# Feed-forward stages of a hybrid encoder layer: all engines but GpSimd in the source's order, a pair's products regrouped, loads two pairs ahead

## The chip, the cores and the metric

The kernel runs on one core of one Trainium2 chip. Times are microseconds on the device, of one execution of the whole layer; lower is better. Five engines work side by side, each with its own queue of instructions: TensorE (PE, with its weight loads as PEld) multiplies matrices, VectorE (DVE) and ScalarE (ACT) do elementwise work, GpSimd (POOL) here raises to a power, copies a little and issues the transfers that add onto their destination, and SyncE (SP) issues the other transfers. They meet only through semaphores: an instruction that waits holds everything behind it on its own engine.

## The reference, cut to what matters

One encoder layer: x is 512 positions by 1024 channels, F is 2752.

```
x = x + 1/2 * SwiGLU_1(RMSNorm(x))
h = RMSNorm(x); u = h @ w_in
x = x + concat([fourier(u), attention(u)]) @ w_out
x = x + 1/2 * SwiGLU_2(RMSNorm(x))
y = RMSNorm_final(x)

SwiGLU(h) = (silu(h @ w_gate) * (h @ w_up)) @ w_down
```

The change touches the two SwiGLU networks alone. Each holds three matrix products of 512 x 1024 x 2752 (gate, up, down).

## The kernel before, in words

Everything is float32, computed as a high part (rounded to the type fp32r that TensorE takes at full rate) and a low remainder; a product is three matmuls: high x high, high x low, low x high. So each weight block that comes in is first cast by ScalarE (the high part) and then subtracted by VectorE (the low part, `lows`, L119).

F is cut into 21 blocks of 128 columns and a tail of 64. Block j of gate and block j of up make pair j. Of each network the first three or four pairs and the tail ("plain", function `gate`, L272) are multiplied in the usual way. The other 17 or 18 pairs go through `seven`, L379: gate and up of a pair are the two column halves of one product, and this product is done in Strassen's manner (Winograd's form) with seven half-sized products in place of eight. For these, VectorE first builds sums of the weight quarters (a11, a12, a22 are quarters; s1 to s4 are sums of them, L368) and, once per network, of the activations (b11 to t4, `operands`, L297). One of the seven products is 12 matmuls of 128 x 256 (`multiply`, L389). Results land in three half banks per pair, called r, q and p: r takes a11, then s2, then s3, then a22, each added onto what is there, and between them ScalarE copies the value out (`kept`, L402, the copy is L404); q takes s1, then s4; p takes a12.

In `seven` the order on TensorE is a11, a12, a22 of the pair before, s1, s2, s4, s3 (`step` 0, 1, 9, 3, 4, 5, 6, L407). `prepare`, L336, issues the loads of the next pair: two half loads into tile s (L344, L345), gate into raw_g (L346), an adding transfer from GpSimd that adds up onto s (L347), and the second half of up into raw_u (L348), a buffer of the pool that the down weights also use. Then come six steps of conversion, of which `PIECES` says how many follow each product: casts of raw_g and s (`both`, L351, cast at L353), of raw_u (`single`, L359, cast at L362), sums, cast of the new s. Tiles raw_g and s have two buffers each. The loads of a pair are issued at the first product of the pair before it.

High and low parts lie in a ring of 12 slots; a slot is taken in the source's order and becomes free when the last product of its quarter is done (`take`, `give`, L325, L331).

At the end of a pair (`step` 9, L436) r is evacuated, gate goes through silu, is multiplied with up and stored as high and low part in `at`, one of seven places (L442, L119).

The network runs in four groups of blocks: group 0 holds the plain pairs, and groups 1 to 3 six or seven blocks each. Before the down products of a group its pairs are multiplied, one block ahead; then, for each of eight blocks d of output channels, the group's part of the down product is done (`down`, L461, 18 matmuls of 128 x 512 for six blocks), added to x with factor 1/2 (`residual`, L481), and the first pair of the next group is prepared alongside (`ahead`). The down weights of block d are loaded and cast when d comes up. The last pair of a group is finished (`rest`) after d = 0.

What sets the order: within `in_order` (L111) the instructions of TensorE and SyncE stand in the order of the source; those of ScalarE, VectorE and GpSimd are placed by the tool's own scheduler, which plays the program through with estimated durations. The mixing stage in between has its order written out by hand for all five engines (`ORDER`, L40).

Of the kernel before, what the change touches and what calls it, by code (L numbers as in the profile page):

```python
# [30 lines left out]
USES = "a11", "a12", "s1", "s2", "s4", "s3", "a22"  # L31
PIECES = (0, 1, 1, 1, 2, 1, 0)
# [48 lines left out]
def encoder(ctx, tc, A, out):  # L81
# [32 lines left out]
    def run(steps):  # L114
        for _, f, a in steps:
            f(*a)
# [134 lines left out]
    def ffn(norm, after, wgu, wd, wdt, groups, opening, closing):  # L251
# [6 lines left out]
        with tc.tile_pool(name=f"act{n_}", bufs=1) as ap, tc.tile_pool(name=f"sums{n_}", bufs=2) as sp:  # L258
# [38 lines left out]
            def operands(rp, i0, i1):  # L297
                for i in range(i0, i1):
# [7 lines left out]
                    t = sp.tile([P, 4, HALF], F32, tag="s", name=f"t{n_}_{i}")  # L306
# [18 lines left out]
            def take():  # L325

                pool = own or shared
                taken.append(pool.pop(0))
                return taken[-1]
# [6 lines left out]
            def prepare(j):  # L336
# [4 lines left out]
                a11, a12, a22 = g[:, :S], g[:, S:], u[:, :S]  # L341
                s3, s1 = s4, s2 = t[:, :S], t[:, S:]
                gate, up = wgu[2 * j], wgu[2 * j + 1]
                nc.sync.dma_start(out=s3.rearrange("p (a b) -> p a b", b=P), in_=gate[:, :KH])  # L344
                nc.sync.dma_start(out=s1.rearrange("p (a b) -> p a b", b=P), in_=up[:, :KH])  # L345
                nc.sync.dma_start(out=g.rearrange("p (a b) -> p a b", b=P), in_=gate)  # L346
                nc.gpsimd.dma_start(out=t.rearrange("p (a b) -> p a b", b=P), in_=up, accum_op=ALU.add)  # L347
                nc.sync.dma_start(out=a22.rearrange("p (a b) -> p a b", b=P), in_=up[:, KH:])  # L348
                w = {}

                def both(names, src):  # L351
                    hi, lo = (take() for _ in range(2))
                    nc.scalar.copy(hi, src)  # L353
                    lows(lo, src, hi)
                    for i, n in enumerate(names):
                        w[n] = tuple(t[:, i * S : (i + 1) * S] for t in (hi, lo))
                    w[max(names, key=USES.index), "slots"] = hi, lo

                def single(n, src):  # L359
                    t = take()  # L360
                    hi, lo = t[:, :S], t[:, S:]
                    nc.scalar.copy(hi, src)  # L362
                    lows(lo, src, hi)
                    w[n] = hi, lo
                    w[n, "slots"] = (t,)

                def add(out, a, b):
                    nc.vector.tensor_tensor(out=out, in0=a, in1=b, op=ALU.add)  # L368

                return w, [  # L370
                    (both, ("a11", "a12"), g),
                    (both, ("s3", "s1"), t),
                    (single, "a22", a22),
                    (add, s2, s1, a11),
                    (add, s4, a12, s2),
                    (both, ("s4", "s2"), t),
                ]

            def seven(js, done):  # L379

                done = [done]
                banks = {}
# [24 lines left out]
                def step(j, w, n):  # L407
                    b = banks.setdefault(j, {})
                    if n == 0:
                        b["r"] = bank(f"r{n_}_{j}")[:, :HALF]  # L410
                        multiply(b["r"], "a11", "b11", w, True, j == js[0])
                        b["p1"] = kept(b["r"], "p1", j)
                    elif n == 1:
                        ps = bank(f"p2{n_}_{j}")[:, :HALF]
                        multiply(ps, "a12", "b21", w, True)
                        b["g"] = tp.tile([P, S], F32, tag="g", name=f"g{n_}_{j}")
                        nc.vector.tensor_tensor(out=b["g"][:, HALF:], in0=ps, in1=b["p1"], op=ALU.add)
                    elif n == 3:
                        b["q"] = bank(f"q{n_}_{j}")[:, :HALF]
                        multiply(b["q"], "s1", "t1", w, True)  # L420
                        b["p5"] = kept(b["q"], "p5", j)
                    elif n == 4:
                        multiply(b["r"], "s2", "t2", w, False)
                        b["u2"] = kept(b["r"], "u2", j)
                    elif n == 5:
                        multiply(b["q"], "s4", "b22", w, False)
                        nc.vector.tensor_tensor(out=b["g"][:, :HALF], in0=b["q"], in1=b["u2"], op=ALU.add)
                        nc.scalar.activation(b["g"], b["g"], AF.Silu)
                    elif n == 6:
                        multiply(b["r"], "s3", "t3", w, False)  # L430
# [15 lines left out]
                for s in range(7 * len(js)):  # L446
                    i, n = divmod(s, 7)
                    if n == 2 and i:
                        step(js[i - 1], done[i - 1][0], 9)
# [37 lines left out]
            for gi, group in enumerate(groups):  # L487
# [64 lines left out]
                for f, *a in ahead:  # L552
                    f(*a)
# [891 lines left out]
```

## Time and profile before

| what | value |
|---|---|
| runs before | 881.05, 882.48, 878.42 us, median 881.05 |
| profiled execution | 876.78 us, of which the span from the first to the last instruction is 875.0 |
| granted TensorE clock, mean | 0.995 |
| TensorE busy in the span | 843.4 us, 96% |
| VectorE, ScalarE, GpSimd busy | 606.8, 468.4, 62.5 us |
| DMA | 116.78 MB, 133 GB/s in the mean |

How to read the lines of the profile: times are microseconds from the start of the span, means of one instruction are nanoseconds. A group's line reads: line of the kernel, engine, operation, tile written <- tiles read, shape, count | busy time, mean of one | idle time of the engine just before, and what ended it. A wait's line reads: engine and line that waited <- what ended the wait: us in total, times, longest. A timeline's line reads: start, length, engine, line, operation, tiles, shape, how many were merged, and in brackets the idle time before and its releaser. A window's line gives the busy time of PE, PEld, DVE, ACT and POOL with their instructions in brackets, the granted clock, the busy share of the DMA engines and GB/s. Matmuls overlap: the start of the next one tells more than the length. The feed-forward networks fill the span up to about 345 us and again from 514 us on; the first pair stage of the first network, for example, runs from 77.6 to 136 us, and the down products after it to 172 us.

### The profile page before, as it was taken

The numbers are of one execution on the slowest core, as the hardware profiler recorded it, in microseconds if no ns is written. First come the engines' busy times: TensorE is split into PE (matmuls) and PEld (weight loads), VectorE is DVE, ScalarE is ACT, GpSimd is POOL, SyncE is SP. The second block draws the span as 40 slices with busy tenths as digits, with TensorE's granted clock in tenths as the row PEclk, the third lists the DMA queues.
The fourth block names the chain that finished last, engine by engine and source line by source line (L and its number), as shares of the span: only waits on it lengthen the run. The fifth ranks groups of instructions, "written<-read, shape, count | busy, mean of one in ns | idle before, by whom it ended". The sixth has DMA issues, their size and how long they took to land.

```text
span 875.0 us, 13923 instructions
## 1 busy us (share of the span) xinstructions
PE 843.4 (96%) x5440; PEld 756.8 (86%) x5440; DVE 606.8 (69%) x937; ACT 468.4 (54%) x781; POOL 62.5 (7%) x70
## 2 busy tenths in 40 slices
PE   9999999999899999999999999999999998999996
PEld 7878988899789998889988888799979997899886
DVE  6986876378646747699997479877745865377453
ACT  7754653266524644677774457366523653266352
POOL 0110000001000000122000001000000000000001
PEclk9999999999999999999999999999999999999998
DMA  6677772757364613414110334787454763747112
GB/s 241 172 161 197 191 202 73 187 141 208 80 185 104 158 55 109 145 49 133 49 49 25 97 105 97 195 193 205 121 159 109 190 159 90 188 125 191 46 61 96
DMA packets 46544, 116.78 MB, mean 133 GB/s; under 512 B 5392, under 2 KB 11024, under 8 KB 46352
## 3 DMA queue, kind: packets, MB, share of 16 engines
q1 hardware_dynamic: 38400, 92.05, 33.2%
q0 software_dynamic: 7536, 23.34, 15.6%
q8 instruction: 42, 0.69, 0.3%
q10 hardware_dynamic: 544, 0.52, 0.2%
q14 instruction: 22, 0.18, 0.1%
HBM read 111.44 MB, written 2.10 MB: 130 GB/s over the span
## 4 chain that ended last, share of the span: by engine, by line
PE 76%; DMA 9%; DVE 6%; ACT 4%; issue 2%; SPq 2%; POOL 0%; POOLq 0%; DVEq 0%; ACTq 0%
PE r L396 14%; PE dn L158 8%; PE dn L157 7%; PE dn L156 7%; DMA raw_u<-in_wgu 7%; PE q L396 6%; PE p L396 4%; DVE ring L119 4%; PE mix L156 3%; PE mix L158 3%; PE mix L157 3%; PE gu L156 3%; PE gu L157 2%; PE gu L158 2%; ACT ring L353 2%
## 5 line engine op out<-in xcount | busy, mean ns | idle before, releaser
L396 PE MATMUL r<-rt,ring 128*128 128x256 f32 x1686 | 212.8, 279 | 12.5 <-ACT u L404 12.4
L396 PEld LDWEIGHTS r<-rt,ring 128*128 128x128 f32 x1686 | 202.4, 189 | 16.0 <-ACT u L404 15.1
L156 PE MATMUL dn<-at,ring 128*128 128x512 f32 x300 | 117.6, 392 | 6.9 <-ACT ring L148 6.9
L158 PE MATMUL dn<-at,ring 128*128 128x512 f32 x300 | 117.8, 393 | 3.4 <-DVE ring L119 3.4
L157 PE MATMUL dn<-at,ring 128*128 128x512 f32 x300 | 116.9, 390 | 0.0
L482 DVE SCALAR_TENSOR_TENSOR gx<-dn,gx 128x512 f32<-128x512 f32 x61 | 42.0, 690 | 96.9 <-PE dn L158 96.9
L396 PE MATMUL q<-rt,ring 128*128 128x256 f32 x840 | 106.7, 276 | 0.0
L353 ACT CAST ring<-s 128x1024 fp32r<-128x1024 f32 x70 | 73.6, 1051 | 61.0 <-PE p L396 26.6
L119 DVE TENSOR_TENSOR ring<-s,ring 128x1024 fp32r<-128x1024 f32 x70 | 85.6, 1223 | 27.1 <-ACT ring L353 26.8
L396 PEld LDWEIGHTS q<-rt,ring 128*128 128x128 f32 x840 | 100.5, 188 | 0.0
L148 ACT CAST ring<-raw_dn 128x768 fp32r<-128x768 f32 (+3 forms) x58 | 45.2, 785 | 92.6 <-PE dn L157 78.0
L156 PEld LDWEIGHTS dn<-at,ring 128*128 128x128 f32 x300 | 56.3, 188 | 19.6 <-ACT ring L148 8.5
L158 PEld LDWEIGHTS dn<-at,ring 128*128 128x128 f32 x300 | 56.3, 188 | 18.7 <-DVE ring L119 7.3
L157 PEld LDWEIGHTS dn<-at,ring 128*128 128x128 f32 x300 | 56.3, 188 | 11.3
L347 POOL DMA_DIRECT2D s<-in_wgu x35 | 30.1, 861 | 466.9 <-DVE ring L119 199.8
L119 DVE TENSOR_TENSOR ring<-raw_dn,ring 128x768 fp32r<-128x768 f32 (+3 forms) x58 | 51.5, 894 | 14.1 <-ACT ring L148 13.0
L119 DVE TENSOR_TENSOR ring<-raw_g,ring 128x1024 fp32r<-128x1024 f32 x35 | 42.9, 1226 | 24.5 <-PE p L396 19.0
L396 PE MATMUL p<-rt,ring 128*128 128x256 f32 x420 | 53.6, 277 | 0.0
L396 PEld LDWEIGHTS p<-rt,ring 128*128 128x128 f32 x420 | 50.6, 189 | 0.0
L353 ACT CAST ring<-raw_g 128x1024 fp32r<-128x1024 f32 x35 | 36.5, 1042 | 21.5 <-DMA raw_g<-in_wgu 20.3
L362 ACT CAST ring<-raw_u 128x512 fp32r<-128x512 f32 x35 | 21.7, 621 | 38.0 <-DMA raw_u<-in_wgu 18.9
L119 DVE TENSOR_TENSOR ring<-raw_u,ring 128x512 fp32r<-128x512 f32 x35 | 24.1, 688 | 16.1 <-ACT ring L362 13.8
(308 smaller groups left out, 1543.0 us busy)
## 6 DMA issues: line engine op xcount, KB each, us to landing
s<-in_wgu SPq DMA_DIRECT2D x70, 256.0 KB, 3.5
raw_g<-in_wgu SPq DMA_DIRECT2D x35, 512.0 KB, 5.3
s<-in_wgu POOLq DMA_DIRECT2D x35, 512.0 KB, 6.2
raw_dn<-in_wd SPq DMA_DIRECT2D x40, 384.0 KB, 3.3
raw_u<-in_wgu SPq DMA_DIRECT2D x35, 256.0 KB, 5.5
raw_gu<-in_wgu SPq DMA_DIRECT2D x12, 512.0 KB, 3.5
raw_o<-in_wo SPq DMA_DIRECT2D x8, 512.0 KB, 3.6
raw_dn<-in_wd SPq DMA_DIRECT2D x8, 448.0 KB, 3.7
```

Source lines behind the costliest of these rows:

```text
L119: nc.vector.tensor_tensor(out=lo, in0=src, in1=asf(hi), op=ALU.subtract)
L148: nc.scalar.copy(hi[:, :n, :], raw[:, :n, :])
L156: nc.tensor.matmul(ps, whi, mhi, start=first, stop=False)
L157: nc.tensor.matmul(ps, whi, mlo, start=False, stop=False)
L158: nc.tensor.matmul(ps, wlo, mhi, start=False, stop=last)
L347: nc.gpsimd.dma_start(out=t.rearrange("p (a b) -> p a b", b=P), in_=up, accum_op=ALU.add)
L353: nc.scalar.copy(hi, src)
L362: nc.scalar.copy(hi, src)
L396: nc.tensor.matmul(ps[:, c], a[:, ks], b[:, i, c], start=first and i == 0 and o == 0, stop=i == KH - 1 and o == 2, skip_group_check=not fi ...
L482: nc.vector.scalar_tensor_tensor(out=x[d][:, t], in0=ps[:, t], scalar=0.5, in1=x[d][:, t], op0=ALU.mult, op1=ALU.add)
```

## The change

All of it lies in `ffn`, in `evacuate`, and in one parameter of the program.

Order: `in_full_order` puts ScalarE and VectorE into the source's order as well, in the pair stages and in the loop over d of every group. GpSimd stays with the scheduler. The source is rewritten so that casts and remainders are calls of their own (`Pair.high`, `Pair.low`) and stand between the products where they are to run.

Products: a pair's order on TensorE becomes a11, s1, a12, s2, a22 of the pair before, s4, s3.

Loads: pair i + 2 is loaded at the first product of pair i. Tile s gets a third buffer, raw_u two buffers of its own of half the size. The area for the descriptors of GpSimd's transfers is halved to 8192 bytes.

Down weights: those of d = 0 are cast inside the last pair (`tail(0)`), those of d = 1 after its last product (`tail(1)`), the others two to four blocks ahead (`more_downs`). Some pairs near the end of a stage take slots of the shared part of the ring first (`late`), so that these are free in time.

Groups: in the loop over d the next group's first pair is loaded at d = 0 and its second at d = 4; the first is converted in five portions at d = 3 to 7 (`steps`). The left-over plain pair of group 0 is evacuated in three parts at d = 0, 1 and 2 (`yield` in `evacuate`).

```
-USES = "a11", "a12", "s1", "s2", "s4", "s3", "a22"
-PIECES = (0, 1, 1, 1, 2, 1, 0)
+USES = "a11", "s1", "a12", "s2", "s4", "s3", "a22"
...
+    def in_full_order():
+        return tc.manual_schedule(engines=ORDERED - {mybir.EngineType.Pool})
...
-                t = sp.tile([P, KD * P], F32, tag="s", name=f"s{n_}_{j}")
-                u = wp.tile([P, KD * P], F32, tag="raw", name=f"raw_u{n_}_{j}")
+                t = sp.tile([P, KD * P], F32, tag="s", bufs=3, name=f"s{n_}_{j}")
...
+                def rest():
+                    u = sp.tile([P, S], F32, tag="raw_u", name=f"raw_u{n_}_{j}")
+                    nc.sync.dma_start(out=blocks(u), in_=up[:, KH:])
...
+                def steps(self):
+                    return [
+                        (),
+                        (),
+                        (),
+                        (self.first_high, lambda: self.low("a11")),
+                        (self.last_high, lambda: self.low("a22")),
+                        (self.sums_high, lambda: self.low("s3")),
+                        (self.more_sums, self.more_high),
+                        (lambda: self.low("s4"),),
+                    ]
...
+                late = {i: names for i, names in ((n - 4, ("s3",)), (n - 3, ("a11",)), (n - 2, ("s3", "s4")))}
...
+                for i, j in enumerate(js):
+                    if i + 2 < n:
+                        pairs.append(Pair(js[i + 2], late.get(i + 2, ())))
+                    p, b = pairs[i], Bank(j, pairs[i].w)
+                    x_ = pairs[i + 1] if i + 1 < n else None
+                    b.p1()
+                    if old:
+                        old.r_rest()
+                        p.low("s4")
+                        p.low("a22")
+                    if i + 2 < n:
+                        pairs[i + 2].load_rest()
+                    b.p5()
+                    if x_:
+                        x_.first_high()
+                        x_.sums_high()
+                    else:
+                        tail(0)
+                    b.p2()
+                    if x_:
+                        x_.low("a11")
+                        x_.low("s3")
+                        x_.more_sums()
+                    b.u2()
+                    if old:
+                        old.last()
+                    if x_:
+                        x_.last_high()
+                        x_.more_high()
+                    if old:
+                        old.both()
+                    b.q()
+                    if old:
+                        old.store()
+                    b.silu()
+                    b.r()
+                    old = b
+                old.r_rest()
+                tail(1)
...
+                more_downs(2 if gi else 3)
+                with in_full_order():
+                    for d in range(KD):
...
+                        if not last and d in (0, 4):
+                            new = Pair(groups[gi + 1][0] + 1 + d // 4)
+                            new.load_rest()
...
+                            residual(d_, ps, every)
+                        more_downs(d + (3 if gi and not last else 4))
+                        if not gi:
+                            next(left_over, None)
+                        elif d == 0:
+                            rest()
+                        for d_, *_ in waiting:
+                            added(d_)
...
-    nc = bacc.Bacc("TRN2", target_bir_lowering=False, num_devices=1)
+    nc = bacc.Bacc("TRN2", target_bir_lowering=False, num_devices=1, dynamic_dma_scratch_size=8192)
```

In the new loop `p1`, `p5`, `p2`, `u2`, `last`, `q` and `r` are the products of a11, s1, a12, s2, a22, s4 and s3 with their evacuation, `both` the product of gate and up, `store` the cast and remainder into `at`, `r_rest` the subtraction that ends the first half of up.

More of the change, by code (lines that the diff above doesn't have):

```diff
@@ L367, in add, with blocks @@
[L367 to L382, printed above, removed]
+                def blocks(t):
+                    return t.rearrange("p (a b) -> p a b", b=P)
```

248 lines of the change are left out of this document (131 added, 117 removed).

## The prediction, on record before the result

> **What bounds the kernel now.** I read the page's first two lines, then TensorE's own waits, then the timeline around the longest of them.
>
> ```profile
> span 875.0 us, 13923 instructions
> PE 843.4 (96%) x5440; PEld 756.8 (86%) x5440; DVE 606.8 (69%) x937; ACT 468.4 (54%) x781; POOL 62.5 (7%) x70
> ```
> ```profile
> PE r L396 <- ACT u L404: 12.4, 10, 2.2
> PE dn L156 <- ACT ring L148: 6.9, 7, 1.2
> PE dn L158 <- DVE ring L119: 3.4, 9, 0.7
> PE dn L158 <- DVE at L119: 0.7, 1, 0.7
> ```
>
> PE is busy 843.4 of 875.0 us, so the most that an order of work can win is the idle remainder, and nearly all of it has these four names: 12.4 + 6.9 + 3.4 + 0.7 = 23.4 us in 10 + 7 + 9 + 1 = 27 waits, all in the feed-forward stages. What one wait costs stands in the PE timeline (start, length, columns as on the page, idle before):
>
> ```profile
> 110.78 1.52 PE L396 MATMUL r<-rt,ring 128*128 128x256 f32 x12
> 112.14 1.52 PE L396 MATMUL q<-rt,ring 128*128 128x256 f32 x12
> 115.81 3.01 PE L396 MATMUL r<-rt,ring 128*128 128x256 f32 x24 [2.15 <-ACT u L404]
> 118.66 1.52 PE L396 MATMUL p<-rt,ring 128*128 128x256 f32 x12
> ```
>
> Undisturbed products of 12 matmuls start every 112.14 - 110.78 = 1.36 us. The third row should have started at 113.50 and started at 115.81, and the one after it (two products later, 2.72 us) at 118.66 instead of 116.22: 2.44 us are lost for an idle time shown as 2.15. So each wait costs its idle time plus 0.29 us (the pipeline's end and refill), and the 27 waits cost 23.4 + 27 x 0.29 = 31.2 us.
>
> What ends this wait is read on ScalarE, and then in the chain that ended last:
>
> ```profile
> 110.98 0.37 ACT L404 COPY p<-q 128x256 f32<-128x256 f32 x1 [0.57 <-PE q L396]
> 114.35 0.62 ACT L362 CAST ring<-raw_u 128x512 fp32r<-128x512 f32 x1 [3.00 <-DMA raw_u<-in_wgu]
> 114.88 0.61 ACT L442 CAST at<-u 128x512 fp32r<-128x512 f32 x1
> 115.40 0.37 ACT L404 COPY u<-r 128x256 f32<-128x256 f32 x1
> ```
> ```profile
> 107.74 6.59 DMA raw_u<-in_wgu
> ```
>
> The copy that PE needs (u<-r, 115.40) stands behind the cast of raw_u and one more, and the cast of raw_u waited 3.00 us for a load issued at 107.74, 6.59 us before. Nothing but its place in ScalarE's queue ties the copy to the load. The second kind of wait is at the passage from the pairs to the down products:
>
> ```profile
> 228.69 1.52 PE L396 MATMUL r<-rt,ring 128*128 128x256 f32 x12
> 231.41 0.50 PE L156 MATMUL dn<-at,ring 128*128 128x512 f32 x1 [1.19 <-ACT ring L148]
> 232.40 0.50 PE L158 MATMUL dn<-at,ring 128*128 128x512 f32 x1 [0.26 <-DVE ring L119]
> 236.16 1.58 PE L396 MATMUL r<-rt,ring 128*128 128x256 f32 x12
> 238.54 0.50 PE L156 MATMUL dn<-at,ring 128*128 128x512 f32 x1 [0.80 <-ACT ring L148]
> 239.53 0.50 PE L158 MATMUL dn<-at,ring 128*128 128x512 f32 x1 [0.26 <-DVE ring L119]
> ```
> ```profile
> 230.53 0.82 ACT L148 CAST ring<-raw_dn 128x768 fp32r<-128x768 f32 x1
> 237.66 0.83 ACT L148 CAST ring<-raw_dn 128x768 fp32r<-128x768 f32 x1 [0.69 <-PE r L396]
> ```
>
> Casts of the down weights run at 230.53 and 237.66, the moment the products that need them should begin; their VectorE remainders cost the two 0.26 us gaps.
>
> A third, hidden loss follows one wait:
>
> ```profile
> 704.03 4.40 PE L396 MATMUL r<-rt,ring 128*128 128x256 f32 x24 [1.83 <-ACT u L404]
> 708.23 1.78 PE L396 MATMUL p<-rt,ring 128*128 128x256 f32 x12
> ```
> ```profile
> 705.40:708.70 3.30, 3.30 (x18) 3.30 (x17) 1.70 (x3) 2.23 (x5) 0.00 (x0) 0.50 0.36 85
> ```
>
> After an idle 1.83 us the granted clock (the column 0.50) is half in this stretch. The 24 matmuls hold up the next product for 708.23 - 704.03 = 4.20 us, where after the wait shown above it was 118.66 - 115.81 = 2.85, and the 12 after them take 1.78 instead of 1.52: 1.35 + 0.26 = 1.6 us.
>
> **The change, part by part.**
> Work is neither added nor removed: the same products, casts, remainders and loads. What moves:
>
> Loads two pairs ahead, own buffers for raw_u, a third for s. A pair's period is 7 x 1.36 = 9.52 us. In the new order SyncE can issue a pair's s loads once the s4 remainder of the pair three before is done, its g once the sums of the pair two before are done, its raw_u once that pair's a22 remainder is done. By the loop worked out below (the fixed order), the sums end about 8.5 us into a period and the cast of g, two periods on, starts about 3 us into its own: 1.0 + 9.52 + 3 = 13.5 us of lead; raw_u has about the same, s more. The load seen took 6.59 us. SyncE's queue waits in this order too (raw_u of one pair stands ahead of s and g of the next, and of the first down weights), but each of those waits ends at least a period before anything behind it is needed; past the end of a stage nothing holds the queue, so the first two pairs of the next stage are loaded during the down products. GpSimd's accumulating loads keep their order. So the 10 waits for a copy go: 12.4 + 10 x 0.29 = 15.3 us. If the cover went, each pair would pay up to the 2.44 us shown.
>
> Down weights: cast and remainder of d = 0 stand inside the last pair, of d = 1 behind its last product, the others two or three d ahead. One d of six blocks is 18 matmuls; 16 of them take from 232.40 to 236.16, 0.23 each, so a d lasts 4.1 us, and a cast and its remainder need 0.82 + 0.96 (next fence). That takes away 6.9 + 3.4 + 0.7 + 17 x 0.29 = 15.9 us. Their cover is the product of the d before; without it 0.82 + 0.96 = 1.8 us for a stage come back.
>
> Source order on ScalarE and VectorE: here sits the price. These engines now do a pair's work in one fixed sequence, and a loop closes over both. The rows:
>
> ```profile
> L417 DVE TENSOR_TENSOR g<-p,p 128x256 f32<-128x256 f32 x35 | 14.8, 421 | 3.6 <-PE p L396 2.8
> L119 DVE TENSOR_TENSOR ring<-raw_g,ring 128x1024 fp32r<-128x1024 f32 x35 | 42.9, 1226 | 24.5 <-PE p L396 19.0 <-ACT ring L353 5.5
> L119 DVE TENSOR_TENSOR ring<-s,ring 128x1024 fp32r<-128x1024 f32 x70 | 85.6, 1223 | 27.1 <-ACT ring L353 26.8
> L368 DVE TENSOR_TENSOR s<-raw_g,s 128x512 f32<-128x512 f32 x35 | 24.2, 691 | 1.0
> L368 DVE TENSOR_TENSOR s<-s,raw_g 128x512 f32<-128x512 f32 x35 | 24.0, 687 | 0.2
> L353 ACT CAST ring<-s 128x1024 fp32r<-128x1024 f32 x70 | 73.6, 1051 | 61.0 <-PE p L396 26.6 <-PE q L396 15.0 <-DMA s<-in_wgu 10.1
> L442 ACT CAST at<-u 128x512 fp32r<-128x512 f32 x35 | 21.7, 621 | 16.1 <-DVE u L441 15.1
> L428 ACT ACTIVATE g<-g 128x512 f32<-128x512 f32 x35 | 21.9, 627 | 0.0
> L432 ACT ACTIVATE u<-r 128x256 f32<-128x256 f32 x35 | 13.0, 372 | 0.2
> L433 DVE TENSOR_TENSOR u<-u,p 128x256 f32<-128x256 f32 x35 | 14.7, 421 | 7.3 <-ACT u L432 7.3
> L119 DVE TENSOR_TENSOR ring<-raw_u,ring 128x512 fp32r<-128x512 f32 x35 | 24.1, 688 | 16.1 <-ACT ring L362 13.8 <-PE dn L157 2.3
> L482 DVE SCALAR_TENSOR_TENSOR gx<-dn,gx 128x512 f32<-128x512 f32 x61 | 42.0, 690 | 96.9 <-PE dn L158 96.9
> L119 DVE TENSOR_TENSOR ring<-raw_dn,ring 128x768 fp32r<-128x768 f32 x40 | 38.1, 958 | 8.1 <-ACT ring L148 7.2 <-PE r L396 1.0
> ```
> ```profile
> 211.18:220.70 9.52, 9.52 (x86) 9.52 (x86) 7.63 (x11) 6.24 (x11) 0.86 (x1) 1.00 0.80 204
> ```
>
> VectorE from the addition that takes the a12 product out of its bank: 0.421 + 1.226 (a11 low) + 1.223 (s3 low) + 0.687 + 0.691 (sums) = 4.25; then ScalarE 1.051 (s4 cast) + 0.621 (store cast) + 0.627 (silu) + 0.372 (u) = 2.67; then VectorE 0.421 (u rest) + 1.223 (s4 low) + 0.688 (a22 low) = 2.33, and then the next such addition. Together 9.25 us against a period of 9.52: it fits with 0.27 us to spare by full durations, more by the starts, since queued instructions overlap a little. The last row is one undisturbed pair: VectorE 7.63 and ScalarE 6.24 of 9.52 us. If the loop lags, PE feels it only at the s2 product, which needs the s4 remainder three products (4.08 us) into the pair. The a12 product of a pair also ends 4.08 us in, and its addition can start 0.20 later (as the copy at 110.98 follows the product that ends at 110.78): 4.28 + 4.25 + 2.67 + 0.42 + 1.22 - 9.52 = 3.3 us into the next pair, 0.75 us early. So I cost the fixed order at nothing between these two ends: a loop shorter than the period, as the last row has it, and the loop of rival B.
>
> Product order. a11 s1 a12 s2 leaves two products (2.72 us) between a11 and s2, which adds onto the bank that ScalarE must copy first; before there were three. The copy takes 0.37 us and starts 0.20 us after its product, so two do. And a22 of the pair before now stands between s2 and s3: two products instead of one (s4) cover the copy that was late ten times. Only the first pair of each of the six stages keeps one.
>
> Left-over evacuation in parts, first pair's preparation spread over d = 3 to 7: in the second network's first stage a d has only 8 matmuls (8 x 0.23 = 1.84 us). VectorE has there 8 x 0.69 (L482) of residuals, 5 x 0.42 of down remainders (128x256, as L433), 4 x 0.69 of evacuation (128x512, as L368) and 1.226 + 2 x 1.223 + 0.688 + 0.687 + 0.691 for the pair, 16.1 us in all, between the end of d = 0 and the s2 product: 7 x 1.84 + 4.08 = 17.0 us. It just fits; I leave 0.5 us. For the start of each of the six stages, where one product less covers everything, I leave 0.25 us: 1.5. Order and time of the mixing stage, of the first gate and up products and of the closing products stay.
>
> The halved descriptor area for GpSimd's transfers: no row prices it. GpSimd issues one such load in 9.52 us and is busy 62.5 us in all by the page's parts; at worst a load would wait for the one before to land, a delay of about 6.59 us, which 13.5 us of lead hide: 0. The end above is a load late in one pair of each stage, 6 x 2.44 = 15 us; below there is no gain.
>
> The row with the clock at 0.50 counts 1.6 us for the dip as a consequence of the wait. [...] I go by the row, since nothing else stands near it.
>
> Sum: -15.3 - 15.9 - 1.6 + 0.5 + 1.5 = -30.8 us. The profiled execution took 876.78 us (span 875.0), so 846 us; it lies 4.3 us under the median of the runs (881.05), hence 881.05 - 30.8 = 850.3, say 851 us as a median. Bounds: with no stall left and none new -32.8, 848; with a new wait as short as the smallest now (0.26 + 0.29) in each of the 35 pairs, +19, 870.
>
> **Rivals.**
> A. Half the gain: the loads come in time, but the fixed order makes a small wait in most of the 35 pairs, each as long as one copy (0.37 us). 35 x 0.37 = 13 us back: 864. For it: the loop is 0.27 us from its bound. Against: 0.75 us of slack before PE sees it, and stages of five or six pairs, too short for a small lag to add up.
> B. Slower: the loop, not PE, sets the pace. Place: the s4 remainder ahead of s2. If a turn takes L us instead of 9.25, the five later pairs of each of six stages lose 5 x (L - 9.52) - 0.75. It eats the 32.8 us at L = 10.8 (5 x 1.25 - 0.75 = 5.5 a stage); at L = 11.0 the time is 851 + 6 x 6.65 = 891 us. For it: eleven instructions in a row, each able to wait behind something foreign on a queue in fixed order. Against: a hand-over is short (the copy at 115.40 ends at 115.77, PE starts at 115.81), so 1.5 us more in a turn of three hand-overs is not in sight.
> C. The change does not reach the stalls: loads are still late, since DMA is 0.80 busy in the pair shown, and the waits move from raw_u to raw_g or s. Then only the passages gain: 881 - 16 = 865, or less.
>
> **How the numbers follow.** Forecast 0.75, A 0.08, C 0.07, B 0.10. Forecast's own range is 845 to 860; with A and C the range is 843 to 872. A measurement of this kernel tells about 0.5% (4.4 us) from no change. Faster: forecast, A and most of C, 0.88; same: 0.03; slower: 0.09.
>
> **What would show it.** In the changed profile: PE's waits for ACT u (copy) and ACT ring (down cast) gone or under 3 us together, PE busy near 843.4 - 27 x 0.29 - 1.6 = 834 us in a span near 844; the cast of raw_u never waiting for a DMA; no half clock between 60 and 830 us; VectorE's busy time unchanged at 607 us, so its share near 72%. The prediction is wrong if PE waits for VectorE's ring remainder at s2 in every pair (B), if ScalarE's casts wait for raw_g or s loads (C), or if the copy still releases PE (A).

## The result, and the profile after

| what | before | after |
|---|---|---|
| median of the first runs | 880.8 us (878.4 to 882.5, 4 runs) | 843.3 us (843.0 to 846.0, 4 runs) |
| ratio, 95% interval | | 0.958 (0.955 to 0.961) |
| a later session, one chip | 878.4 us (873.9 to 884.6, 17 runs) | 842.8 us (842.5 to 844.9, 6 runs) |
| profiled execution, span | 876.8, 875.0 us | 843.4, 841.6 us |

The changed kernel is faster by 37.5 us in the first runs and by 35.6 us in the later session; 851 us was forecast, in a range of 843 to 872. The span of the profiled executions fell by 33.4 us, TensorE's idle time from 31.6 to 8.5 us. First the busy times on the page of the changed kernel, then all of TensorE's waits:

```profile
PE 833.1 (99%) x5440; PEld 754.1 (90%) x5440; DVE 606.9 (72%) x937; ACT 464.3 (55%) x781; POOL 63.5 (8%) x70
```
```profile
PE busy L685 <- DVE halves L715: 1.0, 1, 1.0
PE rp L228 <- POOL r L223: 0.6, 1, 0.6
PE r L429 <- DVE ring L117: 0.5, 1, 0.5
```

All 27 waits in the feed-forward stages are gone, and one new one has come: 0.5 us for a VectorE remainder in the first pair of the second network's first pair stage. The other two stand ahead of the first stage and behind the last, as before. Line 429 is now the multiplication of the seven products, L437 the kept copy, L374 the cast, L117 the remainder. A steady pair on ScalarE, and a passage on TensorE (start, length, idle before):

```profile
188.90 0.37 ACT L437 COPY u<-r 128x256 f32<-128x256 f32 x1 [0.45 <-PE r L429]
...
190.54 0.62 ACT L374 CAST ring<-raw_u 128x512 fp32r<-128x512 f32 x1
```
```profile
219.98 1.52 PE L429 MATMUL r<-rt,ring 128*128 128x256 f32 x12
221.34 0.39 PE L154 MATMUL dn<-at,ring 128*128 128x512 f32 x1
```

The copy of r (188.90) waits for its product and for nothing else, the cast of raw_u (190.54) for nothing at all, and at 221.34 the down products follow the pairs after 1.36 us, the length of one undisturbed product. From the warm-up to the closing stage the clock is full (the column 1.00 behind POOL's busy time):

```profile
5.20:838.00 832.80, 828.94 (x5431) 752.39 (x5429) 605.12 (x929) 462.08 (x777) 62.77 (x64) 1.00 0.50 138
```

### The profile page after: what moved, and what is told of

Read it like the earlier page. It is cut to its first block, busy times and chain, and to the rows that moved or that the text cites. A ratio compares the mean times of both kernels' runs of the same rounds, so it can differ in the third digit from the quotient of the medians.

```text
span 841.6 us, 13753 instructions
## 1 busy us (share of the span) xinstructions
PE 833.1 (99%) x5440; PEld 754.1 (90%) x5440; DVE 606.9 (72%) x937; ACT 464.3 (55%) x781; POOL 63.5 (8%) x70
## 4 chain that ended last, share of the span: by engine, by line
PE 97%; DVE 1%; DMA 1%; issue 0%; ACT 0%; POOL 0%; POOLq 0%; DVEq 0%; ACTq 0%
PE r L429 23%; PE q L429 11%; PE dn L155 8%; PE dn L154 8%; PE dn L156 8%; PE p L429 5%; PE mix L154 4%; PE mix L156 3%; PE mix L155 3%; PE gu L746 3%; PE gu L154 3%; PE gu L155 3%; PE gu L156 3%; PE mix L1236 2%; PE mix L1193 2%; PE mix L1042 1%
## 5 line engine op out<-in xcount | busy, mean ns | idle before, releaser
L429 PE MATMUL r<-rt,ring 128*128 128x256 f32 x1686 | 205.3, 276 | 0.5 <-DVE ring L117 0.5
L429 PEld LDWEIGHTS r<-rt,ring 128*128 128x128 f32 x1686 | 198.6, 188 | 1.6 <-DVE ring L117 0.7
L429 PE MATMUL q<-rt,ring 128*128 128x256 f32 x840 | 106.6, 276 | 0.0
L374 ACT CAST ring<-s 128x1024 fp32r<-128x1024 f32 x70 | 73.5, 1050 | 51.5 <-DVE s L394 51.5
L429 PEld LDWEIGHTS q<-rt,ring 128*128 128x128 f32 x840 | 100.5, 188 | 0.0
L117 DVE TENSOR_TENSOR ring<-s,ring 128x1024 fp32r<-128x1024 f32 x70 | 85.3, 1218 | 0.6 <-ACT ring L374 0.5
L154 PEld LDWEIGHTS dn<-at,ring 128*128 128x128 f32 x300 | 56.3, 188 | 11.3
L117 DVE TENSOR_TENSOR ring<-raw_dn,ring 128x768 fp32r<-128x768 f32 (+3 forms) x58 | 51.7, 895 | 8.0 <-ACT ring L146 7.7
L429 PE MATMUL p<-rt,ring 128*128 128x256 f32 x420 | 53.4, 276 | 0.0
L429 PEld LDWEIGHTS p<-rt,ring 128*128 128x128 f32 x420 | 50.3, 188 | 0.0
L117 DVE TENSOR_TENSOR ring<-raw_g,ring 128x1024 fp32r<-128x1024 f32 x35 | 42.6, 1217 | 0.0
L117 DVE TENSOR_TENSOR at<-u,at 128x512 fp32r<-128x512 f32 x35 | 24.2, 692 | 20.2 <-ACT at L484 20.2
L472 DVE TENSOR_TENSOR u<-g,u 128x512 f32<-128x512 f32 x35 | 24.0, 687 | 19.8 <-ACT u L469 19.8
L374 ACT CAST ring<-raw_g 128x1024 fp32r<-128x1024 f32 x35 | 36.8, 1051 | 0.0
```

The costliest lines, as they stand in the source:

```text
L117: nc.vector.tensor_tensor(out=lo, in0=src, in1=asf(hi), op=ALU.subtract)
L154: nc.tensor.matmul(ps, whi, mhi, start=first, stop=False)
L374: nc.scalar.copy(ts[0], src)
L429: nc.tensor.matmul(ps[:, c], a[:, ks], b[:, i, c], start=first and i == 0 and o == 0, stop=i == KH - 1 and o == 2, skip_group_check=not fi ...
L472: nc.vector.tensor_tensor(out=self["u"], in0=self["g"], in1=self["u"], op=ALU.mult)
```

## The experiments

**The order of products taken back.** Diff against the changed kernel:

```
                     b.p1()
...
+                    b.p2()
+                    if old:
+                        old.last()
                     b.p5()
                     if x_:
                         x_.first_high()
                         x_.sums_high()
                     else:
                         tail(0)
-                    b.p2()
...
                     b.u2()
-                    if old:
-                        old.last()
```

> The changed kernel with the products of a pair in the order of before (a11, a12, a22 of the pair before, s1, s2, s4, s3); loads, buffers, fixed order and down weights stay as changed. Theory (the copy of r was late because it stood on ScalarE behind a cast that waited for a load; the order of the products gave nothing): the time of the changed kernel, 843 us, to within 2 us, and no wait of TensorE for ACT u from the copy in more than one pair of a stage. Rival (the order of the products gives the copy its cover, since now only s4 stands between s2 and s3): waits for the copy in many of the 35 pairs. Ten like those of before bring back 8 to 15 us, 851 to 858 us; 0.37 us and the restart of 0.29 in each of the 35 pairs bring 23 us, 866.

875.5 us (874.8 to 876.1, 10 runs), ratio to before 0.996 (0.994 to 0.998): nearly the whole gain is gone, more than even the rival said. TensorE's waits, then ScalarE and TensorE in one turn:

```profile
PE r L429 <- ACT u L490: 14.9, 28, 0.7
```
```profile
207.84 0.37 ACT L437 COPY p<-q 128x256 f32<-128x256 f32 x1 [0.97 <-PE q L429]
208.11 1.05 ACT L374 CAST ring<-raw_g 128x1024 fp32r<-128x1024 f32 x1
...
213.04 1.05 ACT L374 CAST ring<-s 128x1024 fp32r<-128x1024 f32 x1 [2.14 <-DVE s L394]
...
215.05 0.37 ACT L490 ACTIVATE u<-r 128x256 f32<-128x256 f32 x1
```
```profile
204.79 1.65 PE L429 MATMUL r<-rt,ring 128*128 128x256 f32 x12 [0.67 <-ACT u L490]
...
215.47 1.69 PE L429 MATMUL r<-rt,ring 128*128 128x256 f32 x12 [0.53 <-ACT u L490]
```

It is not the copy that is late, but the evacuation of r (L490), in 28 pairs. A loop has closed that runs through TensorE: the a22 product (204.79), s1 behind it, the copy of s1's result (207.84), the cast of raw_g behind that copy in ScalarE's fixed order (208.11), remainders and sums on VectorE, the cast of the sums (213.04), the store and silu, the evacuation (215.05), and only then the next a22 (215.47). A turn takes 215.47 - 204.79 = 10.68 us against 9.52. So the fixed order can be the bound, as rival B had it, but by another loop than the one I had summed.

**The same, with the casts behind a12.** In that kernel the casts of the next pair (`first_high`, `sums_high`) move from behind `b.p5()` to behind `b.p2()`, where a12 is the second product.

> The changed kernel with the order of products of before, as in the first such run, but with the casts of the next pair's weights put behind a12, the second product, instead of behind s1, the fourth. In the first run these casts stood behind the copy of s1's result on ScalarE, and a turn ran through s1, cast, remainders, sums, cast of s4, silu, evacuation of r, and the a22 product, 10.67 us long. Theory (it was the place of the casts in the fixed order, not the order of the products, that cost 32 us): the casts come 2.7 us earlier, the evacuation of r is done before a22 needs it, 843 to 848 us. Rival (the order of products itself matters under a fixed order: a22 two products earlier needs the evacuation of r two products earlier, and ScalarE's last instructions of a pair cannot be so early): waits for ACT u at the evacuation stay in most pairs, 855 to 876 us.

842.8 us (842.2 to 845.1, 4 runs), ratio 0.958 (0.955 to 0.960): the time of the changed kernel. TensorE has no wait left in the stages of pairs and of down products. The evacuation of r is done 2.1 us before a22 needs it:

```profile
183.75 0.37 ACT L490 ACTIVATE u<-r 128x256 f32<-128x256 f32 x1
```
```profile
186.20 1.52 PE L429 MATMUL r<-rt,ring 128*128 128x256 f32 x12
```

So the new order of products brings nothing that the old one would not; what counts under the fixed order is that the casts stand behind the second product, whichever that is, and not behind the fourth. Both kernels once more, side by side:

> The changed kernel once more, beside the next one, on one chip: 843 us. The kernel before spread over 878 to 882 us in its first runs, 4 us of which the prediction added to the profiled time; if that spread hangs on waits for loads, which the changed kernel does not have, its own runs lie within 1 us of each other but for single ones.

> The changed kernel with the old order of products and the early casts once more: 842 to 843 us, as its one profile (842.2 against 843.4 us) has 1.2 us less than the changed kernel's. The first pair stage of the second network, where the changed kernel has its one wait of 0.5 us for the s4 remainder, is 55.90 us long as the others. If the difference is real, its runs lie 0.5 to 1.2 us under those of the changed kernel; if it is noise, they are equal.

842.8 us (842.5 to 844.9) and 843.4 us (842.4 to 843.6): no difference. Neither order beats the other.

**The new order of products alone**, in the kernel before (steps 0, 3, 1, 4, 9, 5, 6; `USES` to match).

> The kernel before with the new order of a pair's products alone (a11, s1, a12, s2, a22 of the pair before, s4, s3); loads, buffers, scheduler and down weights as before. Theory (the copies were late by the loads, the order of the products only adds cover): s2 to s3 now has two products between, 1.36 us more cover for each of the ten late copies, so a wait of up to 2.2 us shrinks to at most 0.8, while the s1 and a11 copies have one product less of it: 0 to 8 us of gain, 873 to 881 us, and the passages unchanged. Rival (the order of the products is the cure of the copy waits): all ten copy waits and the dip go, 864 us. Second rival (less lead for the s1 weights, which are now needed one or two products earlier, makes new waits for their cast or remainder): over 885 us.

898.3 us (890.9 to 901.0, 3 runs; a fourth took 905.4), ratio 1.020 (1.011 to 1.029): the second rival's time, but the waits are for a copy:

```profile
PE r L396 <- ACT p L404: 17.7, 11, 3.2
```
```profile
99.55 1.05 ACT L353 CAST ring<-raw_g 128x1024 fp32r<-128x1024 f32 x1 [3.47 <-DMA raw_g<-in_wgu]
...
103.59 0.37 ACT L404 COPY p<-r 128x256 f32<-128x256 f32 x1
```

Only two products now stand between a11 and s2, and the copy of a11's result (103.59) still stands behind casts, of which one waits 3.47 us for a load (99.55). With less cover each late copy costs more: 17.7 us in 11 waits, against 12.4 us in 10 before. That is 5 us of the 21.6 by which the span is longer. The waits for casts and remainders of the down weights grow by 6 us (8.9 and 7.4 us against 6.9 and 3.4), and the mean granted clock is 0.988 instead of 0.995. By an estimate from these two means and the spans of 896.6 and 875.0 us, 0.012 x 896.6 - 0.005 x 875.0 = 6.4 us more of the full clock are lost.

**The new buffers alone**, in the kernel before:

```
-                u = wp.tile([P, KD * P], F32, tag="raw", name=f"raw_u{n_}_{j}")
+                u = sp.tile([P, S], F32, tag="raw_u", name=f"raw_u{n_}_{j}")
```

with `bufs=3` for s and the descriptor area of 8192 bytes.

> The kernel before with the new buffers alone: a third buffer for s, raw_u in two buffers of its own instead of the pool shared with the down weights, the descriptor area halved. Loads are still issued one pair ahead. Theory (raw_u came late because its buffer came free late): the waits of the cast of raw_u for its DMA go, with them the ten copy waits and the half clock, 15 to 17 us of the 37 us; the passages to the down products stay: 862 to 866 us against 880.8. Rival (the buffers alone move nothing, since the loads are issued at the same point of the source and SyncE stands in the source's order): 878 to 883 us and the copy waits as before.

876.1 us (873.5 to 883.1, 10 runs), ratio 0.997 (0.994 to 1.000). My theory falls: eight copy waits are left (6.4 and 2.3 us), and ScalarE still waits for loads:

```profile
PE q L396 <- ACT p L404: 6.4, 4, 3.0
...
PE r L396 <- ACT u L404: 2.3, 4, 0.7
```
```profile
ACT ring L362 <- DMA raw_u<-in_wgu: 20.2, 11, 3.5
```

**The buffers and the loads two pairs ahead**, still in the kernel before (`prepare` cut into a load, called for i + 2, and a conversion).

> The kernel before with the new buffers and the loads issued two pairs ahead (the second pair of a stage still at the first product of the first), nothing else: products, scheduler, places of the casts, down weights and left-over evacuation as before. It prices the copy term by itself. Theory (copies are late because a cast ahead of them on ScalarE waits for a load, and a load two pairs ahead is never late but for the second pair of a stage): of the ten copy waits of before at most one in each stage is left and there is no half clock in a pair stage; the passages to the down products stay: 17 us less the second pairs' waits, 863 to 870 us. Rival (the early down weights and the spread preparation of the first pair took the copy waits away in the run with loads and downs, not the lead of the loads): 875 to 881 us with the copy waits as in the run with the new buffers alone, eight in number.

872.9 us (868.8 to 881.0, 10 runs), ratio 0.994 (0.991 to 0.998). Thirteen copy waits, in a profiled execution that took 878.9 us, 6 more than the median, and so may show more of them than a middling run has:

```profile
PE q L405 <- ACT p L413: 8.5, 7, 4.4
...
PE r L405 <- ACT u L413: 4.1, 6, 0.7
```
```profile
204.88 0.62 ACT L370 CAST ring<-raw_u 128x512 fp32r<-128x512 f32 x1 [2.32 <-DMA raw_u<-in_wgu]
...
206.36 0.61 ACT L370 CAST ring<-raw_u 128x512 fp32r<-128x512 f32 x1
...
207.15 0.36 ACT L413 COPY p<-q 128x256 f32<-128x256 f32 x1
```
```profile
198.98 0.59 SPq L350 DMA_DIRECT2D raw_u<-in_wgu  x1
```

Two casts of raw_u, so of two different pairs, stand ahead of a copy (207.15), and the first waits 2.32 us for a load that was issued 5.9 us before. At this place the scheduler has used the earlier loads to put a cast further ahead, and the copy is still behind a cast that waits. Two of the thirteen waits are of another kind. They stand in the first pair of a network's first pair stage, and the longer is the longest of all:

```profile
580.06 1.04 ACT L361 CAST ring<-s 128x1024 fp32r<-128x1024 f32 x1 [6.68 <-DMA s<-in_wgu]
```
```profile
581.43 2.93 PE L405 MATMUL q<-rt,ring 128*128 128x256 f32 x12 [4.38 <-ACT p L413]
```

The copy here stands behind a cast of s that waits for its load, since the source of this kernel still issues the next loads at the first product of that pair. These two, 4.38 and 0.99 us, are what the theory had allowed for; the other eleven, 7.2 us together, it had not. The theory and the rival both miss: 5 us came of the 17.

**Loads, places and down weights, without the fixed order and with the old products** (the kernel of the first experiment, with `in_full_order` returning `in_order()`).

> The changed kernel with the order of products of before and with ScalarE and VectorE left to the scheduler: what is left of the change is the loads two pairs ahead with their buffers, the early down weights and the parts of the left-over evacuation. Theory of the prediction (the copies were late only because a cast ahead of them waited for a load): the ten copy waits go, 15 us; with the 10.5 us that the scheduler's order cost in the run with the new products (7.5 us of it at the start of the second network's pairs), 850 to 858 us. Rival (two products or one between a copy and its user decides, loads or not): the copy waits stay, with the passages better, 862 to 870 us. Second rival (early loads do nothing by themselves): above 872 us.

850.5 us (849.6 to 851.0), ratio 0.966 (0.964 to 0.968), as the theory's number: 30 of the 37 us without a fixed order on ScalarE and VectorE, and not one copy wait. What is left is one place:

```profile
PE dn L154 <- ACT ring L146: 2.6, 1, 2.6
PE dn L156 <- DVE ring L117: 2.0, 1, 2.0
```
```profile
545.41 1.04 ACT L374 CAST ring<-s 128x1024 fp32r<-128x1024 f32 x1 [6.06 <-issue]
546.37 1.04 ACT L374 CAST ring<-raw_g 128x1024 fp32r<-128x1024 f32 x1
547.31 0.61 ACT L374 CAST ring<-raw_u 128x512 fp32r<-128x512 f32 x1
547.83 0.40 ACT L146 CAST ring<-raw_dn 128x256 fp32r<-128x256 f32 x1
```

In the second network's first stage the scheduler put three casts of the next pair ahead of the down cast (547.83). This stage's down products last from 540.11 to 562.68, 22.6 us, and 14.9 us in the changed kernel; part of the difference is a slower TensorE behind these waits: from 551.63 to 555.90 its matmuls start every 0.43 us, from 540.11 to 545.32 every 0.23 us.

**The fixed order taken back, the new products kept** (`in_full_order` returning `in_order()` in the changed kernel).

> The changed kernel with ScalarE and VectorE of the feed-forward stages left to the tool's scheduler again; product order, loads, buffers and the source's early down casts stay as changed. Theory (the loads two pairs ahead take away the cause of the late copies, and the source's order matters only where the scheduler would put a cast behind a load that is late): within 3 us of the changed kernel, 843 to 846 us, with small waits left at passages. Rival (the fixed order itself brings the gain, because the scheduler places instructions by estimated durations and puts casts ahead of copies whatever the loads do): waits for ACT u and ACT ring are back, 855 to 875 us.

853.8 us (852.9 to 854.3), ratio 0.972 (0.968 to 0.976), between the two. The longest waits are at the same place, and four short waits for a copy are back (two of them, for `ACT p L437`, 0.4 us together):

```profile
PE dn L154 <- ACT ring L146: 2.5, 1, 2.5
PE dn L156 <- DVE ring L117: 2.0, 1, 2.0
PE r L429 <- ACT u L437: 1.0, 2, 0.7
```

**No early down weights** (`tail` does nothing).

> The changed kernel without the casts of the down weights inside a pair stage: those of d = 0 and d = 1 stand behind the last pair of a stage, the rest as changed. Theory (the passages are a term of their own, hidden only by the early casts): TensorE waits again at the first down product of each of the six stages, for ScalarE's cast (its evacuation 0.37 and the cast 0.82 us after the last product of the pairs, 1.2 us) and for VectorE's remainder (up to 0.96), each with 0.29 us more. That is 1.8 to 2.7 us a stage, 11 to 16 us in all: 854 to 859 us. Rival (the loads two pairs ahead and the free engines at the end of a stage hide the casts wherever they stand in the source): 843 to 845 us.

849.8 us (849.5 to 851.2), ratio 0.966 (0.963 to 0.968): 6.5 us, half of the theory.

```profile
PE dn L154 <- ACT ring L146: 3.8, 3, 1.4
...
PE dn L156 <- DVE ring L117: 0.8, 3, 0.3
```

Three stages wait, not six: 3.8 + 0.8 + 6 x 0.29 = 6.3 us, 2.1 us a stage as priced. These casts stand between two parts of fixed order, where the scheduler is free, and it put them early enough in the other three.

**One remainder twice** (`p.low("s4", 2)`).

> The changed kernel with the s4 remainder of each pair computed twice by VectorE, the second time redundantly, so that VectorE has 1.14 us more to do in each pair, straight ahead of the s2 product. It measures how far the fixed loop over VectorE and ScalarE is from being the bound. By the changed kernel's own rows VectorE waits 0.78 us in a pair for the a12 product and nothing else in the loop gives way, so a turn takes 9.52 - 0.78 + 1.14 = 9.88 us; it lags 0.36 us more in each pair, the slack of 1.1 us ahead of s2 is used up by the doubled remainder itself, and some 29 pairs lose 0.36 us: about 10 us, 852 to 856 us, with TensorE waiting for DVE ring at s2. By the prediction's sum of full durations a turn takes 9.25 + 1.22 = 10.47 us and loses 5 x 0.95 - 0.75 = 4.0 us a stage: 867 us. Rival (VectorE has 28% of idle time, which takes it in): 843 to 845 us.

857.3 us (856.6 to 858.2), ratio 0.974 (0.972 to 0.976). The pair's period, and VectorE ahead of the doubled work in the changed kernel:

```profile
201.34:211.26 9.92, 9.81 (x87) 9.61 (x85) 9.01 (x13) 6.17 (x12) 0.86 (x1) 1.00 0.78 242
```
```profile
185.01 1.22 DVE L117 TENSOR_TENSOR ring<-s,ring 128x1024 fp32r<-128x1024 f32 x1
186.15 0.69 DVE L117 TENSOR_TENSOR ring<-raw_u,ring 128x512 fp32r<-128x512 f32 x1
187.61 0.42 DVE L461 TENSOR_TENSOR g<-p,p 128x256 f32<-128x256 f32 x1 [0.78 <-PE p L429]
```

TensorE's products repeat every 211.26 - 201.34 = 9.92 us, by the changed kernel's rows 9.88 were expected. Without the added 1.14 us the loop is 8.78 us long, and not 9.25. 0.40 us for each of the 35 pairs is 14 us, which is what the run is longer; I had left out the first pair of each stage.

**Two buffers for s** (no `bufs=3`; the loads of pair i + 2 behind `p.low("a22")`).

> The changed kernel without the third buffer for s: the loads of pair i + 2 are issued behind the s4 remainder of pair i, about 3 us into that pair, instead of at its first product; raw_u keeps its two buffers. The sum on record gives 13.5 us of lead for raw_g and raw_u, which hangs on buffers that come free no earlier than that, and more for s. Theory (all loads still have more lead than the load of 6.6 us needs): the same as the changed kernel, 842 to 846 us, with no wait of ScalarE's cast of s for a DMA over 1 us. Rival (the adding transfer, which comes behind two half loads, needs the third buffer, because three transfers one behind the other take 13 us or more): waits for DMA s at the cast of s, and TensorE waits for it at s1: up to 2.4 us in each of 23 pairs, 850 to 880 us.

854.1 us (853.7 to 854.5), ratio 0.972 (0.969 to 0.976): the theory falls, the third buffer, with the earlier loads that it allows, is worth 11 us.

```profile
ACT ring L374 <- DMA s<-in_wgu: 21.2, 13, 3.0
```
```profile
179.95 0.80 SPq L344 DMA_DIRECT2D s<-in_wgu  x2
```
```profile
184.45 0.86 POOL L346 DMA_DIRECT2D s<-in_wgu  x1 [9.31 <-ACT ring L374]
```
```profile
191.24 1.05 ACT L374 CAST ring<-s 128x1024 fp32r<-128x1024 f32 x1 [1.40 <-DMA s<-in_wgu]
```

The two halves are issued at 179.95, the adding transfer, which needs both, 4.5 us later, and ScalarE's cast waits for that one until 191.24: 11.3 us in all. (The profile infers a ScalarE cast as the releaser of the adding transfer; the medians from issue to landing on the pages of the kernels before and after, 3.5 and 4.4 us for a half and 6.2 and 6.3 us for the adding transfer, fit the two one after the other.) For s two transfers one after the other have to fit, not one.

## Why the prediction was right, and where not

**The waits, 32.8 us.** The count and the price (idle time plus 0.29 us) held: all 27 are gone, the half clock with them, one new wait has come, and the span fell by 33.4, where 32.8 less 0.8 for the new wait was to be expected. TensorE's busy time, forecast near 834, is 833.1, VectorE's 606.9. None of the rivals came: no wait behind a copy in the pairs (A), no wait for the loop (B), no cast of a pair's weights that waits for a load (C).

**Where 851 should have been 844.** The measured 843.3 lies at the very edge of the stated range and below the 848 that I had given as the bound with no stall left; that the range still held it is luck. Two terms of the sum were mis-sized. The allowance of +2.0 us for the left-over evacuation and six stage starts measured 0.5 + 0.29 = 0.8 us. And "it lies 4.3 us under the median of the runs" was carried over to the changed kernel, where there is no such distance: its profiled execution took 843.4, its median is 843.3. The spread is that of the kernels that wait for loads: 873.5 to 883.6 us in 19 runs of before, 868.8 to 881.0 and 873.5 to 883.1 in the two kernels built on it with earlier loads or more buffers; 1.3 us in ten runs of the first experiment, which is as slow but waits for its own fixed loop. So I take it that a median run of before had some 4 us more of stalls than the profiled one, and that these went too: 876.8 - 32.8 = 844 us was the sum to make. The clocks of the runs point the same way: of the 43 runs of before whose clock was taken the ten shortest (up to 876.8 us) had a mean granted clock of 0.995 to 0.997, the nine longest (from 881.4 us) 0.990 to 0.994, and the half clock outside the closing stage stands, in the rows of the last section, behind windows in which TensorE was idle for 1.83 us or more. That those 4 us were waits for loads is argued, not shown: only one execution of before was profiled.

**"So the 10 waits for a copy go", by the loads.** They went, but not by the loads alone, which with their buffers bring 5 us. "Nothing but its place in ScalarE's queue ties the copy to the load" named the cause rightly, and the step then mended the load and not the place. What cures it is the lead together with something in the rest of the rewritten source: the new places of the casts, the first two pairs loaded ahead of a stage, the early down weights. With these and the old products no copy was late even with the scheduler, and with the new products four were, by 1.4 us together. Which of these parts does it was not separated.

**Product order, costed as cover.** Two products do cover a copy, and a22 between s2 and s3 was not needed: the old order does as well. What I left out is the link of the two parts: under the fixed order the place of the casts has to fit the order of products, or 32 us are lost.

**The loop, costed at nothing.** Right, with more room than I had: VectorE idles 0.78 us in a steady pair for the a12 product (187.61), so the loop is 9.52 - 0.78 = 8.74 us, which the doubled remainder confirms (8.78). Full durations made it 9.25, since a queued instruction starts some 0.08 us before the one ahead of it ends: the row at 186.15 follows that at 185.01 after 1.14 us, not 1.22. The s4 remainder ends at 186.23, 1.1 us before the s2 product (187.34); I had 0.75.

**Lead of 13.5 us for raw_g.** It measured 13.7: issued at 191.82, cast at 205.49.

```profile
191.82 0.33 SPq L345 DMA_DIRECT2D raw_g<-in_wgu  x1
```
```profile
205.49 1.05 ACT L374 CAST ring<-raw_g 128x1024 fp32r<-128x1024 f32 x1
```

"s more" hid the tightest of the loads: with one buffer less it is late in 13 pairs.

**Passages, 15.9 us.** All went. Their cover was priced at 1.8 us a stage; where it was taken away, it cost 2.1 us in three stages and nothing in the other three.

**The halved descriptor area, costed at nothing.** It was not run alone. The two kernels that had it with the buffers, and with the buffers and loads, lost nothing (876.1 and 872.9 us).

**Source order.** I asked only what it could cost. What it brings is 7.7 us with the old products (850.5 to 842.8) and 10.5 with the new (853.8 to 843.3), most of it at the second network's first stage, where I had counted 16.1 us of VectorE's work in 17.0.

## What to carry to other kernels

A cast that waits for a load held up what stood behind it on its engine: a cast of raw_u that waited 2.32 us stood ahead of the copy at 207.15, and one of s that waited 6.68 us ahead of a copy for which TensorE then waited 4.38 us. Earlier loads alone brought 5 us of 17 here: look whether the order of that engine uses the lead to place more casts ahead of the urgent copy. With a fixed order on several engines, check every loop that it closes, by start-to-start times and with the last instruction of a turn in mind, not only the one through the busiest engine. When all stalls of a kernel go, set the sum against the profiled execution, and do not add a spread that the stalls may have made.

## What the hardware showed beside

In the rows at hand the half clock lies on a grid. In the kernel before it lasts from 705.34 to 708.75, 3.41 us, and comes again at 869.18, in the closing stage: 163.84 us or 48 times 3.413 us after the first start. With the new buffers alone two stretches of 3.41 us at half clock start at 95.27 and 579.96, 484.69 us or 142 times 3.413 us apart. The rows below are windows of 3.41 us laid on such a grid. Of the kernel before (the window that precedes the dip, the dip, and the two that share the longer idle time of 2.15 us), of the kernel with the new buffers alone, of the one with the new products alone, and of the changed kernel with the scheduler's order:

```profile
701.93:705.34 3.41, 1.58 (x14) 1.38 (x13) 2.12 (x4) 2.15 (x4) 0.00 (x0) 1.00 1.00 230
705.34:708.75 3.41, 3.41 (x18) 3.41 (x18) 1.76 (x3) 2.34 (x5) 0.00 (x0) 0.50 0.36 87
111.42:114.83 3.41, 2.24 (x20) 2.04 (x19) 1.02 (x2) 0.48 (x1) 0.86 (x1) 1.00 1.07 303
114.83:118.25 3.42, 2.44 (x21) 2.44 (x22) 3.01 (x5) 2.79 (x6) 0.00 (x0) 1.00 0.76 157
```
```profile
91.86:95.27 3.41, 1.52 (x14) 1.33 (x13) 2.39 (x3) 2.63 (x5) 0.86 (x1) 1.00 0.22 84
95.27:98.68 3.41, 3.41 (x18) 3.24 (x17) 3.15 (x7) 2.15 (x4) 0.00 (x0) 0.50 0.99 160
576.55:579.96 3.41, 1.24 (x10) 1.24 (x11) 1.50 (x2) 1.59 (x3) 0.00 (x0) 1.00 0.92 205
579.96:583.37 3.41, 3.41 (x18) 3.41 (x17) 2.52 (x4) 1.95 (x3) 0.85 (x1) 0.50 0.26 72
```
```profile
240.68:244.09 3.41, 1.66 (x16) 1.47 (x14) 2.57 (x6) 3.09 (x5) 0.00 (x0) 1.00 0.06 22
244.09:247.51 3.42, 3.13 (x13) 2.27 (x14) 0.90 (x2) 0.00 (x0) 0.00 (x0) 1.00 0.40 107
203.14:206.55 3.41, 1.47 (x13) 1.27 (x12) 1.76 (x4) 2.11 (x4) 0.24 (x1) 1.00 0.93 321
206.55:209.96 3.41, 3.41 (x18) 3.41 (x17) 2.26 (x5) 0.37 (x1) 0.62 (x1) 0.50 0.76 160
```
```profile
545.73:549.15 3.42, 1.51 (x7) 0.93 (x5) 1.25 (x2) 2.33 (x3) 0.00 (x0) 1.00 0.09 23
549.15:552.56 3.41, 0.84 (x3) 0.41 (x4) 3.41 (x6) 1.72 (x5) 0.00 (x0) 1.00 0.00 0
552.56:555.97 3.41, 3.41 (x9) 2.65 (x10) 3.41 (x7) 0.40 (x1) 0.00 (x0) 0.50 0.71 204
```

In five windows at full clock TensorE was idle for 1.83, 1.89, 2.17, 1.94 and 2.57 us, and the next is at half clock; after 1.75 us (240.68) it is not, and neither is it after 1.91 us (545.73), the one row out of line. In the kernel before, between the warm-up and the closing stage, the longest idle time in such a window with full clock behind it is 1.59 us (561.98 to 565.39). The idle 2.15 us at 113 fell, by the same count, into two windows, 1.17 and 0.98 us, and the clock stayed full in both and behind them. The closing stage of the kernel before does not fit: from 865.77 to 869.18, with eight matmuls of 2 columns (L211) among others, TensorE was idle for 1.31 us, and the clock is at half from 869.18 on. The dip of the prediction went with its wait: in the changed kernel the clock is at 1.00 from 5.2 to 838.0.

In the type of the high and low parts, fp32r, a 128x256 matmul of the changed kernel is 276 ns long (L429), in bf16 270 ns (L1384), both at the full clock.
